# The down projection of a ConvFFN as seven products of quarters, with weight sums made by accumulating DMA

## The chip, the cores and the metric

The kernel runs on one core of a Trainium2 chip. The core has five engines that run their own instruction streams beside each other: TensorE (PE) multiplies matrices, VectorE (DVE) and ScalarE (ACT) work on elements, GpSimd (POOL) and SyncE (SP) mostly issue transfers here. Sixteen DMA engines move data between memory (HBM) and the core's on-chip memory (SBUF); products are accumulated in PSUM, eight banks of 128 x 512 fp32. The metric is the device time of one execution in microseconds.

## The reference

One decoder layer over 512 tokens of width 1024: a merge of three token mixers, then a ConvFFN, each with RMSNorm before and after. The change is in the ConvFFN and in the norm behind it:

```python
def conv_ffn(h, w_up, conv_w, conv_b, w_down):
    T = h.shape[1]
    up = h @ w_up
    padded = jnp.pad(up, ((0, 0), (CONV_WIDTH - 1, 0), (0, 0)))
    conv = conv_b + conv_w[0] * padded[:, 0:T]
    for i in range(1, CONV_WIDTH):
        conv = conv + conv_w[i] * padded[:, i:i + T]
    gate, val = jnp.split(conv, 2, axis=-1)
    return (jax.nn.gelu(gate, approximate=True) * val) @ w_down
...
        f = conv_ffn(h, ffn_w_up[l], ffn_conv_w[l], ffn_conv_b[l], ffn_w_down[l])
        x = x + rmsnorm(f, norm_ffn_post[l])
```

The down product is (512 x 2816) @ (2816 x 1024).

## The kernel before

**Precision.** Matrix products run in the type F32R, which keeps fewer bits than fp32. Each fp32 operand is therefore split into a high part (an ACT copy that rounds) and a low part (a DVE subtraction): `split` (L67) for weights, L817 and L818 for activations. A product is three matmuls: high x high, high x low, low x high (`mm3`, L101; `d_mm`, L836).

**Weights.** All weights go through one stream. `weight_order` (L35) lists the tiles of 128 x 1024 in the order of use; `weight` (L95) hands out the next and lets `prefetch` (L86) load and split two tiles ahead. There are 2 raw buffers, filled from SP's queue (L64), and 4 pairs of `whi` and `wlo` buffers (`new_w`, L71).

**The up stage** (L784 to L831). `NF` = 22 tiles of 128 channels, each with a gate part and a value part. For each, 2 x 24 matmuls with 512 token columns (`up_mm`, L776) fill two of the four PSUM banks of `psm`; the first `FIRST` = 2 tiles are done in two halves of the tokens. `up_finish` (L812) then makes the convolution (`conv`, L803: one ACT and two DVE operations per part), the Gelu (ACT, L815), the product (DVE, L816), and the high and low parts of the activation, `ah` and `al`, each 22 x 512 values per partition.

**The down stage** (L833 to L867). All eight PSUM banks hold the result, 4 token blocks x 2 column halves. For each of 18 of the 22 k tiles, 24 matmuls go to all eight banks; the last four k tiles are held back so that the token blocks end one after the other. When a block's half is complete, ACT squares and sums it (L856) and DVE multiplies it by the gain (L858); `base_of` (L135) and `rstd_m2` (L121) make the norm's factor from both halves; DVE adds the scaled result to the residual `x1` (L865), and SP's queue stores it (L867). The gain `gpost` is loaded and scaled by POOL at the start of the up stage (L800, L801).

**Order.** The code is written in one order. The framework gives each engine its own list of instructions, worked out before the run and fixed in it, and puts semaphores where one instruction needs another's result or buffer. Each engine, and each queue that issues transfers, works through its list in turn: whatever waits holds up all behind it. A tile's buffer can be filled again when all who read it are done.

## Time and profile before

| What | us |
|---|---|
| median of 3 runs (800.29 to 802.54) | 802.29 |
| the profiled execution | 802.75 |
| its span in the trace | 801.0 |
| up stage, first to last matmul start | 431.9 to 674.1 |
| down product, first to last matmul start | 674.29 to 793.95 |
| from the start of the last matmul to the end of the span | 7.0 |

The span is cut out of the profiled execution, whose own time is 1.75 us longer. Times on the trace count from the span's start. A row of a group of instructions gives the source line, the engine, the operation, the tiles written and read, the shapes and the count; then the busy time in us and the mean duration of one in ns; then how long the engine stood idle ahead of them, and what ended that. A row of a window gives for each engine the busy time and in brackets the number of instructions, in the order PE, PEld (weight loads), DVE, ACT, POOL, then the granted PE clock as a share of full speed, the DMA engines' busy share and GB/s.

### The profile page before, as it was taken

Reading aid. Unit: us, or ns where it says so; the run is one execution under the profiler, and the core shown is the slowest. Engines: PE = TensorE matmul, PEld = TensorE weight load, DVE = VectorE, ACT = ScalarE, POOL = GpSimd, SP = SyncE. Lnnn points to the kernel's source line nnn. Section 1 sums busy time; section 2 is a strip of 40 time slices with the busy share of each in tenths; the row PEclk is TensorE's granted clock in tenths of the full one; section 3 lists DMA queues with packets and bytes.
Section 4 is the critical chain, followed back from the end, with each engine's and each line's share of the span. In section 5 each row is a group of like instructions: output and inputs, shape, how many; then the busy total and the mean of one; then the engine's idle time right before and its main releaser. Section 6 shows DMA issues by size and latency. Waiting matters only on the chain.

```text
span 801.0 us, 9610 instructions
## 1 busy us (share of the span) xinstructions
PE 791.3 (99%) x3748; PEld 655.1 (82%) x3748; DVE 462.2 (58%) x701; ACT 328.3 (41%) x541; POOL 32.9 (4%) x46
## 2 busy tenths in 40 slices
PE   9999999999999999999999999999999999999996
PEld 7899876778887888888889988888888888888885
DVE  6464676368786556545658666655655665221225
ACT  7354644473224342333445544444444444122132
POOL 0100000011413000000000100000000000000000
PEclk9999999999999999999999999999999999999999
DMA  9434211122224213222550233223223223223202
GB/s 339 128 107 138 74 62 60 65 79 79 79 93 132 80 52 106 92 93 79 174 194 28 93 117 106 92 93 105 97 89 105 101 84 106 98 86 106 104 29 105
DMA packets 24781, 81.02 MB, mean 101 GB/s; under 512 B 2976, under 2 KB 3248, under 8 KB 24736
## 3 DMA queue, kind: packets, MB, share of 16 engines
q1 hardware_dynamic: 23760, 77.83, 27.9%
q0 software_dynamic: 832, 2.58, 1.0%
q8 instruction: 29, 0.48, 0.2%
q14 instruction: 16, 0.13, 0.1%
q10 hardware_dynamic: 144, 0.00, 0.0%
HBM read 78.30 MB, written 2.10 MB: 100 GB/s over the span
## 4 chain that ended last, share of the span: by engine, by line
PE 97%; DVE 1%; ACT 1%; issue 1%; DMA 0%; DVEq 0%
PE up L104 10%; PE up L102 10%; PE up L103 10%; PE pj L102 8%; PE pj L104 8%; PE pj L103 8%; PE pd L841 5%; PE pd L842 5%; PE pd L840 5%; PE pq L195 3%; PE py L104 3%; PE py L103 3%; PE py L102 3%; PE pz L723 2%; PE pz L725 2%; PE pz L724 2%
## 5 line engine op out<-in xcount | busy, mean ns | idle before, releaser
L69 DVE TENSOR_TENSOR wlo<-raw,whi 128x1024 fp32r<-128x1024 f32 (+1 forms) x127 | 152.3, 1201 | 201.4 <-ACT whi L68 201.2
L68 ACT CAST whi<-raw 128x1024 fp32r<-128x1024 f32 (+1 forms) x127 | 131.0, 1032 | 232.8 <-PE pj L103 77.9
L102 PE MATMUL up<-h_hi,whi 128*128 128x512 f32 (+1 forms) x384 | 142.8, 372 | 0.0
L103 PE MATMUL up<-h_lo,whi 128*128 128x512 f32 (+1 forms) x384 | 142.6, 371 | 0.0
L104 PE MATMUL up<-h_hi,wlo 128*128 128x512 f32 (+1 forms) x384 | 142.6, 371 | 0.0
L102 PE MATMUL pj<-h_hi,whi 128*128 128x512 f32 x296 | 117.8, 398 | 0.0
L104 PE MATMUL pj<-h_hi,wlo 128*128 128x512 f32 x296 | 116.2, 392 | 0.0
L103 PE MATMUL pj<-h_lo,whi 128*128 128x512 f32 x296 | 115.8, 391 | 0.0
L103 PEld LDWEIGHTS up<-h_lo,whi 128*128 128x128 f32 x384 | 72.3, 188 | 12.6
L104 PEld LDWEIGHTS up<-h_hi,wlo 128*128 128x128 f32 x384 | 72.3, 188 | 12.5
L102 PEld LDWEIGHTS up<-h_hi,whi 128*128 128x128 f32 x384 | 72.3, 188 | 12.3
L841 PE MATMUL pd<-wlo,act_hi 128*128 128x512 f32 x176 | 68.6, 390 | 0.0
L842 PE MATMUL pd<-whi,act_lo 128*128 128x512 f32 x176 | 68.5, 389 | 0.0
L840 PE MATMUL pd<-whi,act_hi 128*128 128x512 f32 x176 | 68.3, 389 | 0.0
L104 PEld LDWEIGHTS pj<-h_hi,wlo 128*128 128x128 f32 x296 | 55.6, 188 | 14.7 <-issue 2.6
L102 PEld LDWEIGHTS pj<-h_hi,whi 128*128 128x128 f32 x296 | 55.8, 188 | 13.4 <-issue 2.6
L103 PEld LDWEIGHTS pj<-h_lo,whi 128*128 128x128 f32 x296 | 55.8, 188 | 12.1 <-issue 1.0
L841 PEld LDWEIGHTS pd<-wlo,act_hi 128*128 128x128 f32 x176 | 33.0, 188 | 7.2 <-DVE wlo L69 0.3
L840 PEld LDWEIGHTS pd<-whi,act_hi 128*128 128x128 f32 x176 | 33.0, 188 | 6.9
L842 PEld LDWEIGHTS pd<-whi,act_lo 128*128 128x128 f32 x176 | 33.0, 188 | 6.7
L817 ACT CAST act_hi<-t 128x512 fp32r<-128x512 f32 x22 | 13.7, 621 | 58.6 <-DVE t L816 58.6
L805 ACT ACTIVATE t<-up,small_sb 128x512 f32<-128x512 f32 x44 | 34.0, 774 | 0.0
(272 smaller groups left out, 1087.7 us busy)
## 6 DMA issues: line engine op xcount, KB each, us to landing
raw<-in_w_up_dram SPq DMA_DIRECT2D x44, 512.0 KB, 3.2
raw<-in_w_tiles_dram SPq DMA_DIRECT2D x37, 512.0 KB, 3.2
raw<-in_w_down_dram SPq DMA_DIRECT2D x22, 512.0 KB, 3.2
raw<-in_w_br_dram SPq DMA_DIRECT2D x12, 512.0 KB, 3.3
raw<-in_w_out_dram SPq DMA_DIRECT2D x8, 512.0 KB, 3.3
raw<-in_w_v_dram SPq DMA_DIRECT2D x8, 328.0 KB, 3.1
xT<-in_xT_dram SPq DMA_DIRECT2D x8, 256.0 KB, 4.5
wfr<-in_w_first_dram SPq DMA_DIRECT2D x8, 256.0 KB, 4.3
```

What stands on the lines that cost most here:

```text
L68: nc.scalar.copy(hi[:, c], raw[:, c])
L69: nc.vector.tensor_sub(lo[:, c], raw[:, c], hi[:, c].bitcast(F32))
L102: nc.tensor.matmul(ps, lh, rh, start=first, stop=False)
L103: nc.tensor.matmul(ps, lh, rl, start=False, stop=False)
L104: nc.tensor.matmul(ps, ll, rh, start=False, stop=last)
L195: nc.tensor.matmul(pq[i], w[:, kc, i * P : (i + 1) * P], h[:, kc, :], start=kc == 0 and n == 0, stop=kc == KC - 1 and n == 2)
L723: nc.tensor.matmul(pz[t][n], mh[:, kc % 4, tk], wh[:, ns], start=kc == 0, stop=False)
L724: nc.tensor.matmul(pz[t][n], mh[:, kc % 4, tk], wl[:, ns], start=False, stop=False)
L805: nc.scalar.activation(t0, ps, AF.Identity, bias=col(C_CB + i), scale=col(C_CW + 2 * 44 + i))
L840: nc.tensor.matmul(pd[t][n], ah[:, kc, tk], wh[:, ns], start=kc == 0, stop=False)
L841: nc.tensor.matmul(pd[t][n], ah[:, kc, tk], wl[:, ns], start=False, stop=False)
L842: nc.tensor.matmul(pd[t][n], al[:, kc, tk], wh[:, ns], start=False, stop=kc == NF - 1)
```

## The change

Tokens, the 2816 inner channels and the 1024 columns are each cut in half, so that the down product becomes 2 x 2 quarters of activations times 2 x 2 quarters of weights. Seven products of sums of quarters take the place of eight products of quarters (Strassen's scheme, in its form by Winograd). Each of the seven has 11 k tiles (`NH`), 256 tokens (2 blocks) and 512 columns.

- **Activation sums** are made by DVE in `up_finish`, as quarters of fp32: `a2`, `ay`. The first product's activation `a11` is stored already split. For this the 22 tiles are taken in the order 0, 11, 1, 12, ..., so that two successive tiles hold the two halves of the inner channels (in `_layout`). The other products' activations are split in groups of up to 4 k tiles during the down stage (`l_split`), into two halves of one buffer.
- **Weight sums** are made by DMA. Six chain tiles `ch` hold a pair of k tiles each (the sixth has one). A first quarter is loaded plainly from SP's queue; after each split of a chain tile (`w_prepare`), `chain_load` adds the next quarter into it, or loads it plainly, by the table `steps`. Of the six later steps, four add and two load. An adding transfer is issued from POOL's queue.
- **The result** is put together from the seven PSUM sums by DVE and ACT in `combine`, called after the first pair of the next product. The seventh product accumulates onto the first one's banks. The lower tokens (blocks 2 and 3) are normed and stored in `lower_token`, at the start of the seventh product; the upper ones in `upper_token`, behind the last matmuls of each.
- **The gain** is loaded and scaled at the start of the down stage, into a part of the buffer that held `h2l`.

```diff
@@ -21,6 +21,8 @@
 VC = 656
+NH = NF // 2
+TH = T // 2
 LEVELS = (64, 32, 16, 8, 4, 2, 1)
@@ -43,7 +45,7 @@
             o.append(("t", T_GATE + GATE_OF[br] * 8 + m))
-    o += [("o", k) for k in range(4)] + [("u", i) for i in range(2 * NF)] + [("d", k) for k in range(NF)]
+    o += [("o", k) for k in range(4)] + [("u", i) for i in range(2 * NF)]
     return o
@@ -78,7 +80,7 @@
-    tabs = {"t": w_tiles, "v": w_v, "b": w_br, "o": w_out, "u": w_up, "d": w_down}
+    tabs = {"t": w_tiles, "v": w_v, "b": w_br, "o": w_out, "u": w_up}
     order = weight_order()
@@ -794,14 +796,13 @@
     with tc.tile_pool(name="fp", bufs=1) as fp:
-        ah = fp.tile([P, NF, T], F32R, tag="ah", name="act_hi")
-        al = fp.tile([P, NF, T], F32R, tag="al", name="act_lo")
-        gpost = fp.tile([P, D], F32, tag="gpost", name="g_ffn_post")
-        nc.gpsimd.dma_start(gpost, g_ffn_post.partition_broadcast(P))
-        nc.gpsimd.tensor_scalar(gpost, gpost, -0.5, None, op0=ALU.mult)
-        def conv(ps, i):
-            t0 = fp.tile([P, T], F32, tag="t0", name="t0", bufs=3)
+        a11 = fp.tile([P, 2, NH, TH], F32R, tag="a11", name="a11")
+        a2 = fp.tile([P, 2, NH, TH], F32, tag="a2", name="a2")
+        ay = fp.tile([P, 4, NH, TH], F32, tag="ay", name="ay")
+        ch = [fp.tile([P, 2 * T], F32, tag=f"ch{p}", name=f"chain{p}") for p in range(4)]
+        def conv(ps, i, keep=False):
+            t0 = (fp.tile([P, T], F32, tag="tk", name="tk", bufs=2) if keep else
+                  fp.tile([P, T], F32, tag="t0", name="t0", bufs=3))
             nc.scalar.activation(t0, ps, AF.Identity, bias=col(C_CB + i), scale=col(C_CW + 2 * 44 + i))
@@ -809,13 +810,57 @@
-        def up_finish(j, pg, pv):
-            tg = conv(pg, 2 * j)
-            tv = conv(pv, 2 * j + 1)
+        kept = {}
+        def up_finish(n, pg, pv):
+            i = n // 2
+            tg = conv(pg, 2 * n, n % 2 == 0)
+            tv = conv(pv, 2 * n + 1)
             nc.scalar.activation(tg, tg, AF.Gelu_apprx_tanh)
-            nc.vector.tensor_mul(tg, tg, tv)
-            nc.scalar.copy(ah[:, j, :], tg)
-            nc.vector.tensor_sub(al[:, j, :], tg, ah[:, j, :].bitcast(F32))
+            if n % 2 == 0:
+                nc.vector.tensor_mul(tg, tg, tv)
+                nc.scalar.copy(a11[:, 0, i, :], tg[:, :TH])
+                nc.vector.tensor_sub(a11[:, 1, i, :], tg[:, :TH], a11[:, 0, i, :].bitcast(F32))
+                nc.vector.tensor_sub(ay[:, 2, i, :], tg[:, TH:], tg[:, :TH])
+                kept[i] = tg
+            else:
+                t0 = kept.pop(i)
+                nc.vector.tensor_mul(a2[:, :, i, :], tg.rearrange("p (h t) -> p h t", h=2),
+                                     tv.rearrange("p (h t) -> p h t", h=2))
+                nc.vector.tensor_sub(ay[:, 0, i, :], t0[:, TH:], a2[:, 1, i, :])
+                nc.vector.tensor_sub(ay[:, 1, i, :], t0[:, :TH], ay[:, 0, i, :])
+                nc.vector.tensor_sub(ay[:, 3, i, :], a2[:, 0, i, :], ay[:, 1, i, :])
+        steps = ((None, (0, 0), False), (ay[:, 0], (0, 1), True), (ay[:, 1], (1, 1), True), (a2[:, 1], (1, 0), True),
+                 (ay[:, 3], (1, 1), False), (ay[:, 2], (0, 1), True), (a2[:, 0], (1, 0), False))
+        pairs = tuple((k, min(k + 2, NH)) for k in range(0, NH, 2))
+        groups = tuple((k, min(k + 4, NH)) for k in range(0, NH, 4))
+        def chain_load(s, p):
+            kh, nh = steps[s][1]
+            k = slice(*pairs[p])
+            c = ch[p][:, : (k.stop - k.start) * T].rearrange("p (k c) -> p k c", c=T)
+            if steps[s][2]:
+                nc.gpsimd.dma_start(c, w_down[kh, nh, :, k, :], accum_op=ALU.add)
+            else:
+                nc.sync.dma_start(c, w_down[kh, nh, :, k, :])
+        todo = [(s, p) for s in range(len(steps)) for p in range(len(pairs))]
+        ready = {}
+        def w_prepare(upto):
+            while len(ready) < min(upto, len(todo)):
+                s, p = todo[len(ready)]
+                k0, k1 = pairs[p]
+                hi, lo = new_w()
+                split(ch[p], hi, lo, slice(0, (k1 - k0) * T))
+                ready[s, p] = hi, lo
+                if s + 1 < len(steps):
+                    chain_load(s + 1, p)
@@ -828,43 +873,129 @@
                 pp.append(ps)
+            if j == NF - 5:
+                for p in range(4):
+                    chain_load(0, p)
+            if j == NF - 1:
+                w_prepare(2)
+                ch += [wp.tile([P, 2 * T], F32, tag="raw", name=f"chain{p}", bufs=2) for p in (4, 5)]
+                for p in (4, 5):
+                    chain_load(0, p)
             up_finish(j, *pp)
-        pd = [[psx.tile([P, T], F32, tag="mx", name=f"pd{t}_{n}") if t < 2 else
-               psm.tile([P, T], F32, tag="mm", name=f"pd{t}_{n}") for n in range(2)] for t in range(NT)]
-        def d_mm(t, kc, wh, wl, ns_=(0, 1)):
-            tk = slice(t * P, (t + 1) * P)
-            for n in ns_:
-                ns = slice(n * T, (n + 1) * T)
-                nc.tensor.matmul(pd[t][n], ah[:, kc, tk], wh[:, ns], start=kc == 0, stop=False)
-                nc.tensor.matmul(pd[t][n], ah[:, kc, tk], wl[:, ns], start=False, stop=False)
-                nc.tensor.matmul(pd[t][n], al[:, kc, tk], wh[:, ns], start=False, stop=kc == NF - 1)
-        for kc in range(NF - 4):
-            wh, wl = weight("d", kc)
-            for t in range(NT):
-                d_mm(t, kc, wh, wl)
-        wd = [weight("d", kc) for kc in range(NF - 4, NF)]
-        for t in range(NT):
-            ssf = fp.tile([P, 2], F32, tag="ssf", name="ssf", bufs=2)
-            fg = []
-            for n in range(2):
-                for kc in range(NF - 4, NF):
-                    d_mm(t, kc, *wd[kc - NF + 4], ns_=(n,))
-                jk = fp.tile([P, T], F32, tag="t0", name="jkf", bufs=3)
-                nc.scalar.activation(jk, pd[t][n], AF.Square, accum_out=ssf[:, n : n + 1])
-                fgn = fp.tile([P, T], F32, tag="fg", name="fg", bufs=2)
-                nc.vector.tensor_mul(fgn, pd[t][n], gpost[:, n * T : (n + 1) * T])
-                fg.append(fgn)
-                if n == 0:
-                    fb = base_of(fp, ssf[:, 0:1], "fb")
-            rf = rstd_m2(fp, ssf[:, 1:2], "rf", fb)
+        lh = hp.tile([P, 2, 2, 4, TH], F32R, tag="hhi", name="lhs")
+        cb = hp.tile([P, 4, 2, T], F32, tag="hlo", name="comb")
+        gpost = cb.rearrange("p i b c -> p i (b c)")[:, 3, :]
+        nc.gpsimd.dma_start(gpost, g_ffn_post.partition_broadcast(P))
+        nc.gpsimd.tensor_scalar(gpost, gpost, -0.5, None, op0=ALU.mult)
+        left = {}
+        def l_split(s, g):
+            k0, k1 = groups[g]
+            h, n = len(left) % 2, k1 - k0
+            src = steps[s][0][:, k0:k1, :]
+            nc.scalar.copy(lh[:, h, 0, :n, :], src)
+            nc.vector.tensor_sub(lh[:, h, 1, :n, :], src, lh[:, h, 0, :n, :].bitcast(F32))
+            left[s, g] = h
+        lgroups = [(s, g) for s in range(1, len(steps)) for g in range(len(groups))]
+        def l_prepare(upto):
+            while len(left) < min(upto, len(lgroups)):
+                l_split(*lgroups[len(left)])
+        def lhs(s, k, part, tb):
+            tk = slice(tb * P, (tb + 1) * P)
+            if s == 0:
+                return a11[:, part, k, tk]
+            return lh[:, left[s, k // 4], part, k % 4, tk]
+        qp = {}
+        def q_mm(s, tb, p):
+            if (s, tb) not in qp:
+                qp[s, tb] = (qp[0, tb] if s == len(steps) - 1 else
+                             psx.tile([P, T], F32, tag="mx", name=f"q{s}_{tb}") if s < 2 else
+                             psm.tile([P, T], F32, tag="mm", name=f"q{s}_{tb}"))
+            ps = qp[s, tb]
+            wh, wl = ready[s, p]
+            k0, k1 = pairs[p]
+            last = s == len(steps) - 1
+            for k in range(k0, k1):
+                c = slice((k - k0) * T, (k - k0 + 1) * T)
+                hi, lo = lhs(s, k, 0, tb), lhs(s, k, 1, tb)
+                nc.tensor.matmul(ps, hi, wh[:, c], start=k == 0 and not last, stop=False, skip_group_check=last)
+                nc.tensor.matmul(ps, hi, wl[:, c], start=False, stop=False, skip_group_check=last)
+                nc.tensor.matmul(ps, lo, wh[:, c], start=False, stop=k == NH - 1, skip_group_check=last)
+        def square(src, ss):
+            jk = fp.tile([P, T], F32, tag="t0", name="jkf", bufs=3)
+            nc.scalar.activation(jk, src, AF.Square, accum_out=ss)
+        ssf = fp.tile([P, NT, 2], F32, tag="ssf", name="ssf")
+        def result(t, rf, fg):
             for n in range(2):
                 ns = slice(n * T, (n + 1) * T)
                 nc.vector.scalar_tensor_tensor(out=x1[:, t, ns], in0=fg[n], scalar=rf, in1=x1[:, t, ns],
                                                op0=ALU.mult, op1=ALU.add)
                 nc.sync.dma_start(out[t, :, ns], x1[:, t, ns])
+        def lower_token(tb):
+            t = tb + 2
+            for n in range(2):
+                square(cb[:, n, tb, :], ssf[:, t, n : n + 1])
+            fb = base_of(fp, ssf[:, t, 0:1], "fb")
+            for n in range(2):
+                nc.vector.tensor_mul(cb[:, n, tb, :], cb[:, n, tb, :], gpost[:, n * T : (n + 1) * T])
+            result(t, rstd_m2(fp, ssf[:, t, 1:2], "rf", fb), [cb[:, n, tb, :] for n in range(2)])
+        def combine(s, tb):
+            q = qp[s, tb]
+            c0, c1, c2 = (cb[:, i, tb, :] for i in range(3))
+            if s == 0:
+                nc.scalar.copy(c0, q)
+            elif s == 2:
+                nc.vector.tensor_sub(c0, q, c0)
+                nc.vector.tensor_add(c1, qp[1, tb], c0)
+            elif s == 3:
+                nc.vector.tensor_sub(c0, q, c0)
+            elif s == 4:
+                nc.vector.tensor_add(c2, q, c1)
+                square(c2, ssf[:, tb, 0:1])
+                nc.vector.tensor_mul(c2, c2, gpost[:, T:])
+            elif s == 5:
+                nc.vector.tensor_add(c1, q, c1)
+                nc.vector.tensor_sub(c0, c0, q)
+                lower_token(tb)
+        def upper_token(tb):
+            q = qp[0, tb]
+            fb = base_of(fp, ssf[:, tb, 0:1], "fb")
+            square(q, ssf[:, tb, 1:2])
+            fg = fp.tile([P, T], F32, tag="t0", name="fg", bufs=3)
+            nc.vector.tensor_mul(fg, q, gpost[:, :T])
+            result(tb, rstd_m2(fp, ssf[:, tb, 1:2], "rf", fb), [fg, cb[:, 2, tb, :]])
+        for s in range(len(steps)):
+            whole = len(pairs) if s < len(steps) - 1 else 3
+            for p in range(whole):
+                w_prepare(s * len(pairs) + p + 3)
+                if p % 2 == 0:
+                    l_prepare((s - 1) * len(groups) + p // 2 + 2 if s else 2)
+                for tb in range(2):
+                    q_mm(s, tb, p)
+                if p == 0 and s:
+                    for tb in range(2):
+                        combine(s - 1, tb)
+        l_prepare(len(lgroups))
+        w_prepare(len(todo))
+        for tb in range(2):
+            for p in range(3, len(pairs)):
+                q_mm(len(steps) - 1, tb, p)
+            upper_token(tb)
@@ -902,9 +1033,9 @@
     a["w_out"] = g["w_out"][0].reshape(KC, P, D)
-    order = [c for j in range(NF) for c in (j, NF + j)]
+    order = [c for i in range(NH) for j in (i, NH + i) for c in (j, NF + j)]
     a["w_up"] = np.stack([tile_cols(g["ffn_w_up"][0], c * P + ar(P)) for c in order])
-    a["w_down"] = g["ffn_w_down"][0].reshape(NF, P, D)
+    a["w_down"] = g["ffn_w_down"][0].reshape(2, NH, P, 2, T).transpose(0, 3, 2, 1, 4)
     a["pool_w"] = np.ascontiguousarray(g["pool_w"][0].transpose(1, 0, 2))
```

## The prediction

> **What bounds the kernel now.** I read the busy shares first, then the chain that ended last, then the stage that is changed: its window, its product tile `pd`, and the groups of VectorE (DVE) and ScalarE (ACT) in it.
>
> ```profile
> PE 791.3 (99%) x3748; PEld 655.1 (82%) x3748; DVE 462.2 (58%) x701; ACT 328.3 (41%) x541; POOL 32.9 (4%) x46
> ...
> PE 97%; DVE 1%; ACT 1%; issue 1%; DMA 0%; DVEq 0%
> ```
> ```profile
> 674.00:794.00 120.00, 120.00 (x530) 99.06 (x529) 36.99 (x52) 28.31 (x39) 0.00 (x0) 1.00 0.25 88
> ```
> ```profile
> L840 PE MATMUL pd<-whi,act_hi x176: 388/389/395, 674.3 to 793.5; 128*128 128x512 f32 x176
> ...
> L842 PE MATMUL pd<-whi,act_lo x176: 388/389/393, 674.7 to 794.0; 128*128 128x512 f32 x176
> ...
>   DVE wlo L69: 0.3, 1
> ```
>
> TensorE (PE) bounds it: 97% of the chain. In the down product it is busy for all of 120 us at granted clock 1.00, beside DVE at 31%, ACT at 24% and DMA at 0.25. I call the stage's start T0 (674.29). The 528 products of `pd` start from 674.29 to 793.95 with one wait of 0.33 us, so one starts every (119.66-0.33)/527 = 0.2264 us. The 0.39 us of a row is its length in the pipeline, not its price.
>
> **What the change removes on PE.** Seven products x 11 k x 2 token blocks x 3 terms = 462 matmuls of the same shape: 66 fewer, 66 x 0.2264 = **-14.9 us**, and the 0.33 us wait before the last token goes with its code. One of the seven products lasts 66 x 0.2264 = 14.9 us, one pair of k 12 x 0.2264 = 2.72 us. Nothing else on PE changes; what is left is whether the others keep up.
>
> **The up stage.** Per pair of tiles PE needs 48 x 0.2264 = 10.9 us.
>
> ```profile
> L69 DVE TENSOR_TENSOR wlo<-raw,whi 128x1024 fp32r<-128x1024 f32 x43 | 52.7, 1224 | 70.2 <-ACT whi L68 70.2
> L808 DVE SCALAR_TENSOR_TENSOR t<-up,small_sb,t 128x510 f32<-128x510 f32 x43 | 32.2, 749 | 1.5
> L806 DVE SCALAR_TENSOR_TENSOR t<-up,small_sb,t 128x511 f32<-128x511 f32 x43 | 32.0, 744 | 0.3 <-ACT t L805 0.3
> L816 DVE TENSOR_TENSOR t<-t,t 128x512 f32<-128x512 f32 x21 | 14.5, 692 | 0.9
> ```
>
> DVE has 2 x 1.22 + 2 x 0.74 + 2 x 0.75 + 2 x 0.69 = 6.8 us per pair. From 0.69 (512 columns) and 1.22 (1024), 256 columns are estimated at 0.42. An even tile then has one 0.69 and two 0.42 (1.5), an odd one 0.69 and three 0.42 (2.0) where there were 1.4: at most 7.4 of 10.9 us. ACT has less. The four early chain loads are 4 x 1.5 us (priced below) in the queue of weight loads, whose tiles are split three tiles (16 us) ahead. I cost the stage at 0; without that cover it would be 11 x (0.1 + 0.6) = 8 us.
>
> **The entry.** At T0 stand in DVE's way the second half of the last convolution, its product and three subtractions (to about T0+4.3), then the splits of weight pair 2, two activation groups (2.5 together) and weight pair 3: 4.3+1.2+2.5+1.2 = 9.2 us, against PE's need for pair 3 at 3 x 2.72 + 0.23 = 8.4. **+0.9 us** (0 to 2).
>
> **Products 1 to 5 on DVE and ACT.**
>
> ```profile
> L69 DVE TENSOR_TENSOR wlo<-raw,whi 128x1024 fp32r<-128x1024 f32 x19 | 23.3, 1225 | 75.3 <-ACT whi L68 75.3
> L865 DVE SCALAR_TENSOR_TENSOR x<-fg,rfr,x 128x512 f32<-128x512 f32 x8 | 5.7, 748 | 0.1
> L858 DVE TENSOR_TENSOR fg<-pd,g_ffn_post 128x512 f32<-128x512 f32 x8 | 5.5, 690 | 8.3 <-ACT jkf L856 8.3
> L130 DVE SCALAR_TENSOR_TENSOR rfa<-rfy,rfv 128x1 f32<-128x1 f32 x4 | 0.9, 220 | 0.1
> L126 DVE TENSOR_SCALAR rfv<-ssf,fb 128x1 f32<-128x1 f32 x4 | 0.8, 204 | 0.0
> ...
> L132 DVE SCALAR_TENSOR_TENSOR rfr<-rfa,rfy 128x1 f32<-128x1 f32 x4 | 0.6, 159 | 0.1
> L128 DVE RECIPROCAL rfy<-rfs 128x1 f32<-128x1 f32 x4 | 0.6, 155 | 0.8 <-ACT rfs L125 0.8
> L137 DVE TENSOR_SCALAR fb<-ssf 128x1 f32<-128x1 f32 x4 | 0.6, 144 | 0.0
> ```
> ```profile
> L68 ACT CAST whi<-raw 128x1024 fp32r<-128x1024 f32 x19 | 20.0, 1055 | 76.0 <-PE pd L842 75.1 <-PE up L103 1.0
> L856 ACT ACTIVATE jkf<-pd 128x512 f32<-128x512 f32 x8 | 4.8, 599 | 13.8 <-PE pd L842 13.8
> L856 ACT ACTIVATION_READ_ACCUMULATOR jkf<-pd 128x1 f32 x8 | 1.6, 194 | 0.0
> L125 ACT ACT_TABLE_LOAD x1 | 1.3, 1283 | 0.0
> ```
>
> DVE per product: weight splits 5 x 1.23 + 0.69 = 6.8, activation splits 2 x 1.23 + 0.96 (768 columns, between 0.69 and 1.23) = 3.4, combining at most 4 x 0.69 = 2.8: 13.0 of 14.9 us. ACT: 5.9 + 2.9 + at most 1.6 = 10.4. A weight pair is split when the buffers used four pairs earlier come free, 8.2 us ahead of its use, and needs 2.3. Hidden: 0, if the chain's data is there.
>
> **The last product.** Product 5 ends as product 6 starts, and its combining carries both lower tokens: per token 2 x 0.69, then 0.14 + 2 x 0.69 + 0.74 of small operations + 2 x 0.75 = 5.1 us, 10.3 for both. Beside it stand the weight splits of pairs 2 to 5 (3 x 1.23 + 0.69 = 4.4) and two activation groups (1.23 + 0.96 = 2.2): 16.9 us of DVE in 14.9 us of PE, and PE wants pairs 4 and 5 after 9.5 and 10.9 us. So the order on DVE decides. It isn't the code's:
>
> ```profile
> 672.67 0.63 ACT L815 ACTIVATE t<-t 128x512 f32<-128x512 f32 x1 [2.12 <-DVE t L808]
> 674.26 1.05 ACT L68 CAST whi<-raw 128x1024 fp32r<-128x1024 f32 x1 [0.95 <-PE up L103]
> 675.22 0.77 ACT L805 ACTIVATE t<-up,small_sb 128x512 f32<-128x512 f32 x1
> ```
>
> The Gelu (L815) ran before the second convolution (L805) that the code puts ahead of it, and a weight cast before that too: what is ready goes first. With this rule, and the earlier line first among ready ones, the split of pair 3 slips into a gap of token 0 (a square root with its 1.28 us table load), but pair 4 waits for both tokens: done at 14.9 us, activation group 2 at 15.9. PE stands from 9.7, takes up at 15.0, waits again to 15.9 and ends at 15.9 + 22 x 0.2264 = 20.9: **+6.0 us**. In the code's order pair 3 waits too: +8.6. With the splits ahead of the tokens: 0.
>
> ```profile
> 798.00:799.00 1.00, 0.00 (x0) 0.00 (x0) 0.00 (x0) 0.00 (x0) 0.00 (x0) 1.00 0.93 346
> 799.00:800.00 1.00, 0.00 (x0) 0.00 (x0) 0.00 (x0) 0.00 (x0) 0.00 (x0) 0.56 0.47 178
> 800.00:801.00 1.00, 0.00 (x0) 0.00 (x0) 0.00 (x0) 0.00 (x0) 0.00 (x0) 0.50 0.00 0
> ```
>
> After the last matmul (794.2) the clock held until about 799.1, then fell to 0.50. A stand of 5.3 us may just reach that; it would double the price of some following matmuls, 0 to 2 us. I take +0.5. The Trainium skill ("TensorE: Matmul & The Clock Gate", Part 1) has the clock halve after an idle window of about 3.4 us and come back after one busy window as long: by that page the stand would cost an estimated 1.7 us. The trace's fall came after 4.9 us.
>
> **The accumulating transfers** are not in the trace at all. The nearest rows, first the stage's own traffic (the DMA view of 674 to 794) and landing, then one transfer from the POOL queue and the scaling behind it:
>
> ```profile
> q1 hardware_dynamic: 3295, 10.48, 24.7%
> ...
> raw<-in_w_down_dram SPq DMA_DIRECT2D x17, 512.0 KB, 3.2
> ```
> ```profile
> g_ffn_post<-in_g_ffn_post_dram POOLq DMA_DIRECT2D x1, 512.0 KB, 4.0
> ```
> ```profile
> 447.12 2.76 POOL L801 TENSOR_SCALAR g_ffn_post<-g_ffn_post 128x1024 f32<-128x1024 f32 x1 [3.46 <-DMA g_ffn_post<-in_g_ffn_post_dram]
> ```
>
> 10.48 MB in 24.7% of 120 us is 353 GB/s: 512 KB occupy the 16 engines for R = 1.5 us, and land 2.5 us later from POOL's queue. An accumulating one also reads its target. Low end: the second read is free, R = 1.5. High end: nothing overlaps and it does both reads in turn, 4.0 + 1.5 = 5.5. I take two plain transfers end to end, **R = 3.0**, because a chain step reads twice what a plain one reads, and writes once.
>
> Only the steps to products 1, 2, 3 and 5 add; those to 4 and 6 are plain loads at 1.5. Each needs its tile split for the step before, so the adds for one product can run while PE works on the one before: 5.5 transfers in 14.9 us, which R = 2.7 fills. POOL's queue also holds the scaling of the gain: it can start at T0, when its tile is free, lands 4.0 later and takes 2.76, so the adds from pair 2 of product 1 on start at T0+7. From there to pair 4 of product 3 they are 3.5 + 5.5 + 5 = 14 in a row: it lands at T0+7+14R+2.5, and must be there 2.3 us ahead of its use at T0 + 3 x 14.9 + 10.9, so by T0+53.4. No stall up to R = 3.13; above, **14 us for each us of R**. The plain loads for product 4 let the queue catch up, and the adds for product 5 (issued from 4.4 us before product 4 starts, needed by 23.5 after it) are in time up to R = 5. With the other terms at -7.8 (below), the gain is used up at R = 3.13 + 7.8/14 = **3.7**. At 3.0 the adds cost 0.
>
> The Trainium skill ("Collectives: The Full Stack", "The bandwidth ceiling") says that a reduction by DMA needs two source reads on one ring, and has 62.28 against 32.35 GB/s, 1.93 to 1. With 1.49 us for a plain 512 KB that is an estimated 2.87, which would leave the sum as it is; a price of 1.5 from the plain rows would too. No run here shows it yet.
>
> **The tail.**
>
> ```profile
> 797.24 1.00 SPq L867 DMA_DIRECT2D out_dram<-x  x2
> ```
>
> From the last matmul (793.95) to the end (801.0) the last token's square, scale, rstd, two updates and store remain as they were: 0.
>
> **Sum,** on the profiled execution (802.75, span 801.0): -14.9 - 0.3 + 0.9 + 6.0 + 0.5 = -7.8, so 794.95; the median of the runs shown, 802.29, is 0.46 lower: **794.5**.
>
> **Rivals.** (1) Everything is hidden: DVE takes the splits first. For it: the readiness order could put them in more gaps. Against: 16.9 us of work in 14.9. It gives 802.3 - 15.2 = 787.0. (2) DMA becomes the bound in products 1 to 3: if the transfers of POOL's queue don't overlap at all, R is a plain one's landing time, 4.0, and the stall is 14 x 0.87 = 12.2 us: 794.5 + 12.2 = 806.7; with the second read behind it, R = 5.5, 33.2 us and some 2.6 in product 5: 830. It decides from R = 3.7. For it: in these products 193 GB/s of sums (5.5 x 0.524 MB in 14.9 us) must come from engines that move 353 plain, on one queue, in chains. Against: the engines have 0.25 of their time taken today, and the six chains are independent of each other. (3) No gain: R near 3.7, or the last product in the code's order with a cold clock, and a later entry: 800 to 804.5.
>
> **Chances.** Forecast 0.52 (own range 790 to 799.5), hidden 0.13, DMA bound 0.24, no gain 0.11. A change of 0.3% (2.4 us) is about what a measurement of this kernel can tell from none. Faster: 0.52 + 0.13 + 0.01 of the last case = 0.66; same 0.07; slower 0.24 + 0.03 = 0.27. The range goes from 787 to R = 4.6 (794.5 + 14 x 1.47 = 815); slower adds (up to 830) and less than 787 are left out, with about 0.15.
>
> **What would show it.** 462 matmuls, 0.226 us apart where nothing is waited for; weight loads of product 6 that wait some 5 us for DVE `wlo` (the line of `split`), with the lower tokens' updates just ahead on DVE; no PE wait above 1 us in products 1 to 5; a DMA share that gives R (1.0 over products 1 and 2 would mean 2.7 or more). If PE waits there, through `whi`, for casts that wait for chain tiles, rival 2 holds. If no wait in product 6 is over 1 us, rival 1. A stall in the up stage would break the sum elsewhere.

## The result, and the profile after

The changed kernel takes 789.55 us (median of 4 runs, 787.93 to 790.02); the kernel before took 801.37 in the same session (4 runs, 800.29 to 802.54; three of them gave the 802.29 that the forecast started from). The ratio is **0.9849** (95% interval 0.9826 to 0.9872): a gain of about 12 us where 7.8 were forecast. That lies in the stated range of 787 to 815, and just under the 790 at which the forecast's own case began. The profiled execution took 789.27 us, its span is 787.5.

The runs of each kernel here fall on two values some 2 us apart, by stages ahead of the down product (its first matmul came at 671.8 in one profile of the changed kernel and at 673.5 in another); so differences of a few us are read below as **D**, the time from the first matmul of the down product to the end of the span. D was 801.0 - 674.29 = 126.7 before and is 787.5 - 673.5 = 114.0 now.

The page of the changed kernel, the busy shares and the chain that ended last:

```profile
PE 775.8 (99%) x3682; PEld 642.3 (82%) x3682; DVE 514.5 (65%) x784; ACT 353.7 (45%) x570; POOL 53.8 (7%) x70
...
PE 95%; DVE 3%; issue 1%; ACT 1%; DMA 0%; DVEq 0%
```

PE has 66 matmuls fewer (3748 to 3682) and still makes the chain. DVE's share of the chain rose from 1% to 3%: in the seventh product the chain runs over DVE's list from 762.8 to 775.4, up to the one wait of 0.5 us shown below, and after the last matmul it runs over DVE again.

Next the busy time by stretches, one line for each product and one for the tail (start and end, length, then PE, PEld, DVE, ACT, POOL, the granted clock, the DMA share, GB/s):

```profile
673.50:688.50 15.00, 15.00 (x68) 12.42 (x67) 11.33 (x14) 8.48 (x10) 7.71 (x7) 1.00 0.76 152
688.50:703.40 14.90, 14.90 (x67) 12.36 (x66) 8.76 (x9) 8.40 (x11) 4.70 (x6) 1.00 1.03 193
703.40:718.40 15.00, 15.00 (x68) 12.40 (x67) 10.31 (x10) 8.68 (x10) 4.02 (x5) 1.00 1.06 218
718.40:733.40 15.00, 15.00 (x68) 12.43 (x67) 12.11 (x14) 8.69 (x10) 1.29 (x2) 1.00 0.70 190
733.40:748.30 14.90, 14.90 (x67) 12.34 (x66) 10.92 (x12) 8.58 (x10) 3.95 (x5) 1.00 0.99 191
748.30:763.30 15.00, 15.00 (x68) 12.43 (x67) 12.12 (x14) 9.91 (x14) 0.00 (x0) 1.00 0.53 169
763.30:778.30 15.00, 14.90 (x65) 11.82 (x64) 14.16 (x30) 8.47 (x16) 0.00 (x0) 1.00 0.19 71
778.30:787.50 9.20, 0.65 (x3) 0.19 (x2) 5.04 (x14) 1.85 (x6) 0.00 (x0) 0.81 0.31 115
```

Six products run without a gap on PE, at full clock, although the DMA engines are taken all the time in the second and third (1.03, 1.06) and in the fifth (0.99). In the seventh, DVE is busy for 14.16 of 15.00 us: the tightest place, as forecast. But PE hardly waits there. The waits of PE's weight loads, from 670 to 790, all of them:

```profile
PEld q L929 <- DVE lhs L898: 0.5, 1, 0.5
PEld q L928 <- DVE wlo L71: 0.3, 1, 0.3
```

By the tile `q`, the down product's matmuls start from 673.5 to 778.57: 105.07 us, 14.6 less than the 119.66 before. Of D's 12.7 the rest is a loss: from the start of the last matmul to the end there are now 787.5 - 778.57 = 8.93 us, where there were 801.0 - 793.95 = 7.05.

### The profile page after: what moved, and what is told of

Read it like the earlier page. It is cut to its first block, busy times and chain, and to the rows that moved or that the text cites. A ratio compares the mean times of both kernels' runs of the same rounds, so it can differ in the third digit from the quotient of the medians.

```text
span 787.5 us, 9695 instructions
## 1 busy us (share of the span) xinstructions
PE 775.8 (99%) x3682; PEld 642.3 (82%) x3682; DVE 514.5 (65%) x784; ACT 353.7 (45%) x570; POOL 53.8 (7%) x70
## 4 chain that ended last, share of the span: by engine, by line
PE 95%; DVE 3%; issue 1%; ACT 1%; DMA 0%; DVEq 0%
PE up L106 10%; PE up L105 10%; PE up L104 10%; PE pj L106 8%; PE pj L104 8%; PE pj L105 8%; PE q L929 4%; PE q L928 4%; PE q L927 4%; PE pq L197 3%; PE py L106 3%; PE py L104 3%; PE py L105 3%; PE pz L725 2%; PE pz L727 2%; PE pz L726 2%
## 5 line engine op out<-in xcount | busy, mean ns | idle before, releaser
L71 DVE TENSOR_TENSOR wlo<-raw,whi 128x1024 fp32r<-128x1024 f32 (+1 forms) x105 | 125.3, 1196 | 126.5 <-ACT whi L70 126.3
L70 ACT CAST whi<-raw 128x1024 fp32r<-128x1024 f32 (+1 forms) x105 | 107.8, 1027 | 185.2 <-PE pj L105 76.8
L106 PEld LDWEIGHTS pj<-h_hi,wlo 128*128 128x128 f32 x296 | 55.6, 188 | 14.5 <-issue 2.6
L71 DVE TENSOR_TENSOR wlo<-chain,whi 128x1024 fp32r<-128x1024 f32 (+1 forms) x42 | 47.4, 1130 | 22.5 <-ACT whi L70 22.5
L70 ACT CAST whi<-chain 128x1024 fp32r<-128x1024 f32 (+1 forms) x42 | 41.2, 981 | 33.4 <-PE q L929 25.6
L848 POOL DMA_DIRECT2D chain<-in_w_down_dram x24 | 21.0, 876 | 465.0 <-DVE wlo L71 464.9
L929 PE MATMUL q<-whi,lhs 128*128 128x512 f32 x132 | 51.5, 390 | 0.1
L928 PE MATMUL q<-wlo,lhs 128*128 128x512 f32 x132 | 51.5, 390 | 0.0
L927 PE MATMUL q<-whi,lhs 128*128 128x512 f32 x132 | 51.4, 389 | 0.0
L652 DVE TENSOR_TENSOR g<-pj,rstd_b 128x512 f32<-128x512 f32 x24 | 16.4, 686 | 30.0 <-PE pj L106 30.0
L929 PEld LDWEIGHTS q<-whi,lhs 128*128 128x128 f32 x132 | 24.8, 188 | 5.6 <-DVE lhs L898 0.5
```

The source lines that it names most:

```text
L70: nc.scalar.copy(hi[:, c], raw[:, c])
L71: nc.vector.tensor_sub(lo[:, c], raw[:, c], hi[:, c].bitcast(F32))
L106: nc.tensor.matmul(ps, ll, rh, start=False, stop=last)
L652: nc.vector.tensor_mul(g1, gates.pop((br, m)), rstd_b)
L848: nc.gpsimd.dma_start(c, w_down[kh, nh, :, k, :], accum_op=ALU.add)
L927: nc.tensor.matmul(ps, hi, wh[:, c], start=k == 0 and not last, stop=False, skip_group_check=last)
```

## The experiments

Four questions were open: why the stall of the seventh product did not come, what is left to gain there, whether the accumulating transfers are truly free, and whether another engine can take work from DVE. All edits are made on the changed kernel; ratios are to the kernel before.

### The lower tokens' last step left out

```diff
@@ combine, s == 5
-                lower_token(tb)
+                for n in range(2):
+                    nc.sync.dma_start(out[tb + 2, :, n * T : (n + 1) * T], x1[:, tb + 2, n * T : (n + 1) * T])
```

> The norm of the lower token blocks (2 and 3) is left out; their residual is stored as it is, at the same place. Theory: the changed kernel's PE loses only 0.8 us to waits in the seventh product, and its tail is 8.9 us instead of 7.1 since the last matmuls of both upper blocks end together; without the lower tokens on VectorE both go, so about 2.5 us less than the changed kernel (ratio to before about 0.982), PE waits in that product under 0.3 us. Rival (the prediction's step): the amount of VectorE work in that product costs some 6 us, so 5 us or more less (ratio 0.979 or below).

Measured: 785.6 us, 0.9802 (0.9784 to 0.9820). Matmuls from 672.0 to 776.5, no wait of a weight load, D = 783.9 - 672.0 = 111.9. What is left out is 7.5 of the 10.3 us of work in the prediction; the four sums of 0.69 stay. This work, and the collision that the prediction priced at 6.0 us, cost **114.0 - 111.9 = 2.1 us** in the changed kernel, as expected.

### Tokens first: the order that the prediction assumed, forced

```diff
+        def behind(c):
+            nc.vector.scalar_tensor_tensor(out=c, in0=x1[:, 3, D - 1 : D], scalar=0.0, in1=c, op0=ALU.mult, op1=ALU.add)
@@ before the split of a weight pair
+                if s == len(steps) - 1 and p > 3:
+                    behind(ch[p][:, 0:1])
@@ before the split of an activation group
+            if s == len(steps) - 1 and g == 2:
+                behind(a2[:, 0, k0, 0:1])
```

> The splits of weight pairs 4 and 5 and of the last activation group of the seventh product are tied behind both lower tokens, the order that the prediction took for granted on VectorE. If PE keeps the code's order (block 0, then block 1), as the prediction had it, PE ends some 6 us later than its ideal, 5 us above the changed kernel (ratio to before about 0.991). Theory now: PE's list is laid out by readiness too, it takes block 1's pair 3 during the wait, so 2 to 3 us above the changed kernel (ratio about 0.988).

Measured: 792.28 us, 0.9885 (0.9865 to 0.9905); D = 117.4, **+3.4**. With pairs 4 and 5 and the last group tied behind both tokens' updates, the stall is there. The waits of the weight loads:

```profile
PEld q L934 <- ACT lhs L904: 3.1, 1, 3.1
```

And the windows of this kernel, one microsecond each, around that stand:

```profile
772.00:773.00 1.00, 0.73 (x4) 0.26 (x2) 1.00 (x2) 0.00 (x0) 0.00 (x0) 1.00 1.04 387
...
775.00:776.00 1.00, 0.55 (x1) 0.50 (x2) 1.00 (x2) 0.92 (x2) 0.00 (x0) 0.63 0.00 0
...
778.00:779.00 1.00, 1.00 (x4) 0.76 (x4) 0.00 (x0) 0.00 (x0) 0.00 (x0) 0.66 0.00 0
779.00:780.00 1.00, 1.00 (x6) 0.82 (x5) 0.00 (x0) 0.23 (x1) 0.00 (x0) 1.00 0.00 0
```

PE stands from 772.73 (0.73 of the first line) to 775.45 (0.55 of the second). The granted clock falls to a half inside the second line (0.63: at 775.26) and comes back inside the third (0.66: at 778.68): 3.4 us at half speed, of which PE worked 3.2, so 1.6 us are lost. The Trainium skill ("TensorE: Matmul & The Clock Gate", Part 1) has the clock come back after one busy window of about 3.4 us, and the trace agrees. So the stall that the prediction described is real, the clock's fall too, but the stand is 2.7 us and not 5.3: PE came to it at about 11 us into the product and not at 9.7, since block 1's pair 3 (6 x 0.2264 = 1.4 us) ran ahead of block 0's pair 4 (by the count: 48 matmuls, pairs 0 to 3 of both blocks, take 10.9 us), and it was relieved after 13.8 us (775.45, the product having begun at 761.6) and not after 15.0.

### Splits first: the lower tokens called behind the last splits

```diff
-                if p == 0 and s:
+                if p == 0 and s and s < len(steps) - 1:
@@ after the last splits
         w_prepare(len(todo))
+        for tb in range(2):
+            combine(len(steps) - 2, tb)
```

> The combining of the sixth product with the lower tokens is called after the last splits in the code, nothing else. Theory: the order on VectorE is worth 0.8 us of PE waits, and with splits in time PE runs block 0 to its end before block 1, so that the tail goes back from 8.9 to about 7.1 us: 2.5 us less than the changed kernel (ratio to before about 0.982). Rival: the lower tokens only move into the tail, so no gain or a loss of up to 2 us.

Measured: 787.45 us, 0.9822 (0.9794 to 0.9849); no wait of a weight load; D = 783.0 - 670.3 = **112.7**, 1.3 less than the changed kernel where 2.5 were expected: the wait is gone, but the tail is 783.0 - 774.8 = 8.2 us and not 7.1. What remains against 111.9 stands at the end. VectorE's timeline there (start, length, instruction), the matmuls being over at 774.8:

```profile
775.52 0.75 DVE L940 SCALAR_TENSOR_TENSOR x<-fg,rfr,x 128x512 f32<-128x512 f32 x1
776.19 0.75 DVE L940 SCALAR_TENSOR_TENSOR x<-comb,rfr,x 128x512 f32<-128x512 f32 x1
776.85 0.68 DVE L979 TENSOR_TENSOR fg<-q,comb 128x512 f32<-128x512 f32 x1
...
778.88 0.74 DVE L940 SCALAR_TENSOR_TENSOR x<-comb,rfr,x 128x512 f32<-128x512 f32 x1
```

The last block's `q` is complete at about 775, but its product with the gain (L979) comes at 776.85, behind two updates of the block before it. The work has moved from the middle of the seventh product to the end, where a part of it shows.

### Plain loads in place of the adding ones

```diff
-                nc.gpsimd.dma_start(c, w_down[kh, nh, :, k, :], accum_op=ALU.add)
+                nc.gpsimd.dma_start(c, w_down[kh, nh, :, k, :])
```

> The adding transfers become plain loads of the same bytes from the same queue, so the weight sums are left out. Theory: the adds are hidden at 2.9 us per 512 KB, so the time stays within 0.3% of the changed kernel, while the DMA share of the second and third product falls from about 1.0 to about 0.55. Rival: the busy DMA engines or the late sums cost PE or VectorE something, then 1 us or more less.

Measured: 789.22 us, 0.9843 (0.9825 to 0.9861), D = 114.0: **no difference**. The DMA view from 660 to 785, of the changed kernel first, then of this one (packets, MB, share of the 16 engines; then the landing):

```profile
q0 software_dynamic: 3600, 12.06, 52.5%
...
chain<-in_w_down_dram POOLq DMA_DIRECT2D x20, 512.0 KB, 7.1
```
```profile
q0 software_dynamic: 3344, 12.06, 30.6%
...
chain<-in_w_down_dram POOLq DMA_DIRECT2D x20, 512.0 KB, 4.1
```

The same 12.06 MB take 52.5% of 125 us with the adds, 184 GB/s, so R = 0.524/0.184 = **2.85 us** for 512 KB; 30.6%, 315 GB/s and 1.66 us without. (Both include the gain's plain load of 0.52 MB; with it taken out, an add needs 2.9 us.) An add lands 7.1 us after its issue where a load lands after 4.1. None of it reaches PE. The estimate from the Trainium skill ("Collectives: The Full Stack", "The bandwidth ceiling"), 2.87, agrees with the measured 2.85. But it was worked out from a plain load of 1.49 us in the kernel before; beside the plain loads of this queue an add costs 2.85 / 1.66 = 1.72 times as much and not 1.93, so part of the agreement is luck.

### Two more steps that add

```diff
-                 (ay[:, 3], (1, 1), False), (ay[:, 2], (0, 1), True), (a2[:, 0], (1, 0), False))
+                 (ay[:, 3], (1, 1), True), (ay[:, 2], (0, 1), True), (a2[:, 0], (1, 0), True))
```

> The steps to the fifth and seventh product add too instead of loading plainly, so those weight sums are others than the reference needs. Theory: at 2.9 us per add the chain needs 15.9 us for a product of 14.9, falls behind by 1 us per product and has some 8 us to spare: no PE wait, time within 0.3% of the changed kernel, DMA share near 1.0 over the whole stage. Rival: the two plain steps are what keeps the chain in time; without them 5 us or more above the changed kernel.

Measured: 788.49 us, 0.9851 (0.9836 to 0.9866), D = 113.7: no difference. The window of its fourth product, where the changed kernel had a DMA share of 0.70:

```profile
716.80:731.80 15.00, 15.00 (x68) 12.43 (x67) 12.12 (x14) 8.68 (x10) 5.28 (x7) 1.00 1.05 191
```

Adds can be had in a row through the whole stage. By the count, 5.5 x 2.85 = 15.7 us of transfers for a product of 14.9 fall behind by 0.8 a product, 4 to 5 us over the stage; the lead with which they begin would cover that, and the next experiment measures this lead.

### The chain started late

```diff
         nc.gpsimd.tensor_scalar(gpost, gpost, -0.5, None, op0=ALU.mult)
+        for _ in range(6):
+            nc.gpsimd.tensor_scalar(gpost, gpost, 1.0, None, op0=ALU.mult)
```

> After the gain is scaled, POOL scales it six times more by 1.0 (2.8 us each), so that the adding transfers behind it in POOL's queue start 10 us (pair 4 of the second product) to 15 us (pair 0 of the third) later than in the changed kernel. Theory: the adds for the second to fourth product are one queue at 2.9 us per 512 KB that has only some 8 us to spare and can't catch up, so the delay shows to its excess: PE waits for casts of chain tiles, 6 to 9 us above the changed kernel (ratio to before about 0.994). Rival: the queue catches up between products, and only the delayed pairs themselves are late: 1 to 3 us (ratio about 0.987).

Measured: 795.57 us, 0.9944 (0.9929 to 0.9959); D = 121.8, **+7.8**. GpSimd's timeline of this kernel, then its waits over the stage:

```profile
679.37 13.31 POOL L892 TENSOR_SCALAR comb<-comb 128x1024 f32<-128x1024 f32 x4
692.63 0.90 POOL L848 DMA_DIRECT2D chain<-in_w_down_dram  x1
...
699.31 6.10 POOL L848 DMA_DIRECT2D chain<-in_w_down_dram  x6
```
```profile
ACT whi L70 <- DMA chain<-in_w_down_dram: 14.0, 9, 4.5
POOL chain L848 <- DMA chain<-in_w_down_dram: 6.3, 3, 3.1
```

The six extra scalings hold the queue from 679.37 to 699.31, 20 us, in which two adds get through; then six stand in a row. The casts wait for transfers (14.0 us in nine waits), the queue can't catch up, since a product's adds take longer than a product, and 7.8 us reach PE. Some of that is the clock. PE's timeline where it first stands, and three windows of this kernel (the last one lies behind the last matmul):

```profile
699.87 0.49 PE L929 MATMUL q<-whi,lhs 128*128 128x512 f32 x1 [1.92 <-ACT lhs L899]
```
```profile
700.00:701.00 1.00, 0.97 (x2) 0.27 (x2) 1.00 (x2) 0.24 (x1) 1.00 (x5) 0.75 0.03 4
...
703.00:704.00 1.00, 1.00 (x4) 0.74 (x4) 0.00 (x0) 0.00 (x0) 1.00 (x3) 0.54 1.05 201
...
789.00:790.00 1.00, 0.00 (x0) 0.00 (x0) 1.00 (x2) 0.00 (x0) 0.00 (x0) 0.62 1.01 377
```

PE stood for 1.92 us, and the granted clock was at a half from 700.50 to 703.92, which costs some 1.6 us. The late transfers alone thus cost about 6.2, and the margin of the changed kernel is between 20 - 2 x 2.85 - 6.2 = 8.1 and 20 - 6.2 = 13.8 us of delay, an estimate that depends on how the delay is counted. The rival by which the transfers become the bound has its mechanism; the kernel is only this far from it.

### The gain multiplied on GpSimd

```diff
@@ lower_token
-                nc.vector.tensor_mul(cb[:, n, tb, :], cb[:, n, tb, :], gpost[:, n * T : (n + 1) * T])
+                nc.gpsimd.tensor_mul(cb[:, n, tb, :], cb[:, n, tb, :], gpost[:, n * T : (n + 1) * T])
```

> The gain's four multiplications for the lower tokens go from VectorE to GpSimd, in the changed kernel's order. Theory: 2.4 us less on VectorE in the seventh product; PE's waits of 0.8 us go, but PE's list still ends both blocks together, so the tail stays near 8.5 us: 1 us less than the changed kernel (ratio to before about 0.984). Rival: the slower GpSimd (1.1 to 1.5 us for one) delays the tokens, no gain.

This expectation failed. Measured: 793.1 us, 0.9909 (0.9894 to 0.9924); D = 117.4, **+3.4** although DVE has four instructions less. GpSimd worked from 768.53 to 775.1 on them (first row); DVE in that time and just behind:

```profile
768.53 6.55 POOL L950 TENSOR_TENSOR comb<-comb 128x512 f32<-128x512 f32 x4 [26.32 <-ACT jkf L933]
```
```profile
769.17 2.26 DVE L71 TENSOR_TENSOR wlo<-chain,whi 128x1024 fp32r<-128x1024 f32 x1
...
772.60 0.13 DVE L139 TENSOR_SCALAR fb<-ssf 128x1 f32<-128x1 f32 x1
772.65 1.20 DVE L134 SCALAR_TENSOR_TENSOR rfr<-rfa,rfy 128x1 f32<-128x1 f32 x1
...
776.34 0.15 DVE L134 SCALAR_TENSOR_TENSOR rfr<-rfa,rfy 128x1 f32<-128x1 f32 x1
776.41 0.94 DVE L898 TENSOR_TENSOR lhs<-a,lhs 128x768 fp32r<-128x768 f32 x1
```

A split (L71) takes 2.26 us where it takes 1.22. One column (L134) takes 1.20 while GpSimd runs and 0.15 after it; L139, with one input, keeps its 0.13 in the same stretch. So what is held is the DVE instruction with two inputs in SBUF, though not every one: in the changed kernel, beside GpSimd's scaling of the gain (677.88 to 680.65), a group's split at 678.16 took 1.83 instead of 1.21, but a product at 679.91 its usual 0.68. This agrees with the Trainium skill ("SBUF — State Buffer", "Who interferes with whom"): a DVE instruction with two SBUF inputs contends with a GpSimd instruction that reads SBUF. The last group's split slips to 776.41, PE stands, and the clock falls again. The windows of this kernel:

```profile
774.00:775.00 1.00, 0.83 (x4) 0.36 (x2) 1.00 (x1) 0.00 (x0) 1.00 (x1) 1.00 0.00 0
...
777.00:778.00 1.00, 0.59 (x3) 0.50 (x4) 1.00 (x3) 0.00 (x0) 0.00 (x0) 0.98 1.01 377
...
781.00:782.00 1.00, 1.00 (x5) 0.82 (x4) 0.00 (x0) 0.18 (x1) 0.00 (x0) 0.81 0.00 0
```

PE stood from 774.83 to 777.41, 2.6 us; the clock was at a half from 777.96 to 781.38, 3.4 us again.

### Splits first and the gain on GpSimd

This is the edit of "splits first" and that of the last experiment together.

> Both the later combining (e3) and the multiplications on GpSimd (e7). Theory: no PE waits, block 0 ends 3.4 us before block 1, and VectorE is done with the lower tokens before the last block: tail 7.1 to 7.6 us instead of 8.9, down stage and tail together near 112 us instead of 114 (ratio to before about 0.980).

This expectation, near 112 us, failed too. Measured: 787.89 us, 0.9852 (0.9836 to 0.9869), D = 114.1. No weight load waits, but a multiplication on GpSimd takes 1.4 to 1.7 us (one pair in a row took 3.38) in the chain of a token that now runs to the end: the tail is 786.1 - 776.5 = 9.6 us. What the splits gain, this gives back.

### The changed kernel and "splits first" again

> The changed kernel once more, beside the two that follow on the same chip: ratio to before about 0.985, as at first.

> The kernel of e3 once more. Theory: 1.3 us (its trace from the start of the down stage, 112.7 against 114.0) to 2.5 us less than the changed kernel beside it (ratio to before 0.982 to 0.984). Rival: the gain of e3 was chance, no difference.

Measured: 787.63 us, 0.9845 (0.9827 to 0.9863), and 787.36, 0.9829 (0.9811 to 0.9847). The intervals overlap: by times alone the two are not told apart. By the traces they are: D was 114.0 and 114.0 in the two profiles of the changed kernel, 112.7 and 112.7 in those of "splits first".

### One token early, one behind the splits

```diff
-                if p == 0 and s:
+                if p == 0 and s and s < len(steps) - 1:
@@ behind the loop over tb
+                if p == 1 and s == len(steps) - 1:
+                    combine(s - 1, 0)
@@ after the last splits
+        combine(len(steps) - 2, 1)
```

> In the seventh product the first lower token's combining is called after the second pair, the other one's after the last splits. Theory: PE's list is that of e3 (block 0 to its end, then block 1), no waits, and VectorE has 1 us less of lower-token work left behind the last matmul: between e3 and 1 us less than e3. Rival: VectorE's total work up to the last update, not its order, sets the end, so no difference to e3.

Measured: 787.18 us, 0.9827 (0.9809 to 0.9845), D = 784.4 - 671.9 = 112.5, with no wait of a weight load. By D, it and "splits first" are the best versions found that compute the whole layer; a difference of 0.2 us of D, with one profile of this kernel, does not rank them.

## Why the prediction was right in sign and short in size

The forecast rested on the 66 matmuls, and these came out as priced. Of the losses that it set against them, +0.9, +6.0 and +0.5, only 0.7 came. By its own sign, "if no wait in product 6 is over 1 us, rival 1", the rival held: the longest wait is 0.5 us. That the time still stands within the stated range is partly luck: the range reached down to this rival's 787.0, and a tail that the prediction put at 0 added 1.9.

Its sum against the traces, step by step (measured: the two profiled executions, 802.75 and 789.27):

| step | forecast, us | measured, us |
|---|---|---|
| 66 matmuls fewer | -14.9 | -14.9: the matmuls of the kernel without the lower tokens' step start over 104.5 us, and 461 x 0.2264 is 104.4 |
| wait before the last token | -0.3 | -0.3 |
| up stage | 0 | no wait of PE; the start of the down product came 0.8 earlier, within what runs of one kernel differ |
| entry | +0.9 | 0: PE busy 15.00 of 15.00; pair 3 was split at 681.7, 8.2 after the start, ahead of work that the prediction put before it |
| products 1 to 5, adds | 0 | 0, at R = 2.85 where 3.0 was taken |
| last product | +6.0 | +0.7 |
| clock after the stand | +0.5 | 0, since there was no stand |
| tail | 0 | +1.9 |
| sum | -7.8 | -13.5 (with the 0.8) |

**Right.** The price of a matmul by the distance of starts, the cover of the adds by the product ahead, and the value of R, for which two plain transfers end to end were the nearest row. The late chain shows that "the adds cost 0" was a matter of a margin and not of indifference. The margin itself, 8 us or more by that estimate, was larger than the prediction's 14 x (3.13 - 2.85) = 3.9 at the measured R.

**Wrong: the step "the last product", with "the entry" and the clock that hang on the same assumption.** It says that the order on DVE decides, and that stands: "tokens first" brings the stall. It then works the order out as: pair 3 slips into a gap of token 0, "but pair 4 waits for both tokens: done at 14.9 us". In the trace nothing waits for both. DVE's timeline of the changed kernel in that product, which begins at 763.3 (the small operations on one column left out, and the sums L970 and L971):

```profile
763.39 1.22 DVE L71 TENSOR_TENSOR wlo<-chain,whi 128x1024 fp32r<-128x1024 f32 x1
764.53 1.22 DVE L898 TENSOR_TENSOR lhs<-a,lhs 128x1024 fp32r<-128x1024 f32 x1
...
767.46 1.22 DVE L71 TENSOR_TENSOR wlo<-chain,whi 128x1024 fp32r<-128x1024 f32 x1
...
770.04 1.28 DVE L950 TENSOR_TENSOR comb<-comb 128x512 f32<-128x512 f32 x2
...
771.75 1.20 DVE L71 TENSOR_TENSOR wlo<-chain,whi 128x1024 fp32r<-128x1024 f32 x1
...
773.08 1.41 DVE L940 SCALAR_TENSOR_TENSOR x<-comb,rfr,x 128x512 f32<-128x512 f32 x2
...
774.47 0.95 DVE L898 TENSOR_TENSOR lhs<-a,lhs 128x768 fp32r<-128x768 f32 x1
775.34 1.41 DVE L940 SCALAR_TENSOR_TENSOR x<-comb,rfr,x 128x512 f32<-128x512 f32 x2
776.66 0.69 DVE L71 TENSOR_TENSOR wlo<-chain,whi 128x512 fp32r<-128x512 f32 x1
```

Pair 3 (767.46) comes after the sums, pair 4 (771.75) between the small operations of the roots, group 2 (774.47) between the two tokens' updates, pair 5 (776.66) behind them. The two tokens run in step with each other and not one after the other, and the splits stand in the seams. Pair 4 ends at 772.95, 9.65 us into the product, where PE wants it after 9.5.

Two more of its terms were off in the same direction. **The work was priced by the rows' durations.** Back to back, DVE instructions start closer than their rows say: 763.39 and 764.53 are 1.14 apart for a row of 1.22, 774.47 and 775.34 are 0.87 apart for one of 0.95. 0.08 for each of the 30 instructions of this window is 2.4 us: the work of 16.9 us ran from 762.79, the first of the sums, to the end of the last split, 777.3, in 14.5. The prediction took exactly this care for PE's matmuls and not for DVE. So its "16.9 us of DVE work in 14.9 us of PE", the ground on which it gave "all hidden" a small chance, was no overload. **PE's own order was taken to be the code's,** all of block 0 and then all of block 1. In the trace the last 30 matmuls of both blocks are interleaved: where one block's operands are late, the other's go. It shows in the order of the lines, which within one block is always L927, L928, L929. PE's timeline:

```profile
774.99 0.39 PE L928 MATMUL q<-wlo,lhs 128*128 128x512 f32 x1
775.48 0.50 PE L929 MATMUL q<-whi,lhs 128*128 128x512 f32 x1
775.82 0.39 PE L927 MATMUL q<-whi,lhs 128*128 128x512 f32 x1
```

This is the longest gap, 0.26 us beyond the usual distance and 0.11 behind it. What the interleaving is worth shows in "tokens first": 1.4 us of the stand.

**Wrong: the tail at 0.** Since PE's list interleaves, both upper blocks end together, and the last steps of two tokens run at the end where there was one. VectorE's timeline from there: the product with the gain of each block (L979, behind ACT's square), and the last updates:

```profile
779.03 0.69 DVE L979 TENSOR_TENSOR fg<-q,comb 128x512 f32<-128x512 f32 x1 [1.56 <-ACT jkf L933]
779.93 0.69 DVE L979 TENSOR_TENSOR fg<-q,comb 128x512 f32<-128x512 f32 x1
...
782.75 0.75 DVE L940 SCALAR_TENSOR_TENSOR x<-fg,rfr,x 128x512 f32<-128x512 f32 x1
783.42 0.74 DVE L940 SCALAR_TENSOR_TENSOR x<-comb,rfr,x 128x512 f32<-128x512 f32 x1
```

The second pair of everything is the price of the order that spares PE its waits: 1.9 us of tail. Why "splits first" has 8.2 us there instead of 8.9 is seen above: its PE list does run block 0 first (the squares of the two blocks start at 771.81 and 775.21, where they start at 778.31 and 779.23 in the changed kernel).

**The rivals.** "Everything is hidden", at 787.0, came closest. It had two reasons: "DVE takes the splits first" is not what happened, and "the readiness order could put them in more gaps" is. The argument against it, the overload, was wrong. "No gain", from 800 up, fell. "DMA bound" fell: R is below its threshold of 3.13, and plain loads change nothing. That the layout of both lists follows readiness is argued from the orders in the traces; what rule breaks ties was not tried.

## What to carry to other kernels

Where two pieces of work meet on an engine, price them by the distance of starts in the trace, as for PE, and take the order on every engine as open: a stall worked out from an assumed order was 6 us in the sum and 0.7 in the trace. Work with slack between its own steps (roots, reciprocals) leaves seams for other work, so call it after what PE waits for. A term that is hidden should have its margin measured too: delay it on purpose until it shows.

## What the runs showed of the hardware

- Transfers that add into SBUF move 184 GB/s where plain ones on the same queue move 315 (2.85 against 1.66 us for 512 KB), land after 7.1 us instead of 4.1, and keep 16 engines at a share of 1.0 without a wait on PE.
- GpSimd reading SBUF can hold DVE instructions with two SBUF inputs: one column took 1.20 us instead of 0.15, a split 2.26 instead of 1.22. Moving work off a full DVE made the kernel slower.
- PE stood for 2.7 us (tokens first), 2.6 us (gain on GpSimd) and 1.9 us (chain late), and the granted clock fell to 0.50, each time for 3.4 us, the last two times only after PE had taken up again; after the end of the kernel before it fell 4.9 us behind the last matmul. The Trainium skill ("TensorE: Matmul & The Clock Gate", Part 1) gives an idle window of about 3.4 us. Here 1.9 us of idle were enough.
- The clock's changes within one trace lie whole multiples of 3.413 us apart: in the late chain it fell at 700.50 and, behind the end, at 789.24, which is 26 x 3.413 later; in the kernel before it fell at 171.06 and at 799.12, 184 x 3.413 apart. So in these traces the clock changes only at places a fixed 3.413 us apart, and a stand counts by how it lies to them. In the 3.413 us ahead of a fall PE was idle for 57% (late chain), 74% (tokens first) and 76% (gain on GpSimd); 27 and 36% in the late chain (703.9 to 710.7), 40% in the kernel before (792.3 to 795.7) and 49% in the changed kernel (777.2 to 780.6) brought none. What is counted is not shown: the fall at 171.06 follows 3.4 us with only 23% idle, in which 16 of the 20 matmuls have two columns.
